# The sample tokens' state updates moved from the GDN and retention mixers into the feed-forward layers behind them

## The chip, the cores and the metric

The kernel runs on one core of a Trainium2 chip. A time is the device time of one execution in microseconds (us). The five engines are TensorE (PE; its weight loads are PEld), VectorE (DVE), ScalarE (ACT), GpSimd (POOL) and SyncE (SP). Each takes its own list of instructions strictly in order, and a DMA is issued by one of these lists.

## The reference

One step of a four-layer decoder over 264 tokens: 256 of a prompt and 8 sample tokens, each of another sequence. The mixers of the layers are pooling, gated DeltaNet (GDN), retention, pooling; behind each stands a SwiGLU feed-forward layer, and each sublayer ends in a layer norm. What the change touches are the new states of the 8 sample tokens, which are outputs:

```python
# GDN, per head (dk = dv = 128) and sample token
S = S * gl_n[..., None, None] + einsum('bhcd,bhce->bhde', kg_n, v_new)
# retention, per head (dk = 128, dv = 256)
S = gC[:, None, None] * S + einsum('bhcd,bhce->bhde', kz_n, v_n)
# feed-forward
a, b = split(x @ w13, 2); y = (silu(a) * b) @ w2
```

For a sample token a chunk is one token, so the new state is the old one times a decay plus an outer product of a key and a value. GDN has 8 heads of 8 states of 128x128 (0.52 MB a head, 4.2 MB in all), retention 8 heads of 8 states of 128x256 (1.05 MB a head, 8.4 MB in all). Nothing later in this step reads the new states; the mixers read the old ones, for the sample tokens' outputs.

## The kernel before

Activations lie with the 1024 features on partitions (8 blocks of 128) and the 264 tokens along the free axis. Each weight comes as float32 in chunks of 1 MB over SP's queue (`chunk`, three `raw` buffers); ACT casts it to a rounded high part (L198), DVE subtracts it from the raw chunk for the low part (L199), and each product is three matmuls (`mm3`, L123): high by high, high by low, low by high. The halves of a chunk have three buffers for each part, and the matmul results four PSUM buffers.

A feed-forward layer (`ffn`) runs over j = 0 to 21 blocks of w13 and then over 11 chunks of w2. The first eight j (`ND`) work on the activations before the layer norm, so that TensorE needn't wait for it. For them the norm is put in afterwards (`unfold`): DVE multiplies the product by 1/sigma (L396), ACT makes a correction u (L395), and POOL adds it (L397). Meanwhile `apply` makes the normed x of each block (L383, DVE L385, POOL L386, L387, L388). `evac` then gives silu(a)*b and its two parts (L413 to L416). The statistics of the norm come once, behind j = 0 (`stats`, L348 to L367): its vv is L355 on DVE. From j = 8 on only L198, L199 and `evac` are left. Here j = 0 to 7 are called the first phase, the rest the second.

In GDN (`sample`, `updates`), ACT's queue loads the states of two heads (`st`); TensorE multiplies each state with the key and the query of its token; `vn` and `vs` (8x128) follow on DVE, and `vs` goes to DRAM (`vd`, L930). `updates` brings `vd` back, one copy for each partition (`vbc`, one buffer, L938). POOL multiplies `st` by the decay (L940), DVE adds key by value with one instruction for each token (L948); for heads 4 to 7 POOL does half of the tokens (L943, L944). SP stores the result. `updates` runs for heads 0 to 3 behind the first half of the chain, woven into projections (`weave`), and for heads 4 to 7 in the output projection.

In retention the same stands in `chain`, per head: ACT multiplies by the decay (L1229), `vbc` comes in two halves (L1232), DVE adds (L1235), SP stores.

A scheduler of the framework places the instructions on each engine by its own timeline of estimated durations, so an instruction can stand far from where the code has it; `keep_in_program_order` fixes an instruction against its neighbours in the code on that engine. A buffer is reused once its last reader is done; for a stored tile that is the end of its store.

## Time and profile before

| | |
|---|---|
| three runs | 1429.88, 1430.71, 1433.75 us; median 1430.71 |
| the profiled execution | 1427.95 us, of it the span 1426.2 us |
| granted TensorE clock, mean | 0.973 |
| busy: PE, DVE, ACT, POOL | 1337.8 (94%), 1069.2 (75%), 821.6 (58%), 477.5 us (33%) |
| moved by DMA | 244.48 MB, of it 210.59 on SP's queue and 32.13 on ACT's; POOL issues none |

PE is busy in nearly the whole span, so a part of the kernel takes as long as its matmuls, plus the time in which they wait, plus what a clock below 1.00 adds. The stages that matter here are GDN with its updates (397 to 500 us), the feed-forward layer of layer 1 (first phase about 530 to 575, second to 700), retention (766 to 945) and the feed-forward layer of layer 2 (first phase about 1000 to 1043, second to 1175).

### The profile page before, as it was taken

The numbers are of one execution on the slowest core, as the hardware profiler recorded it, in microseconds if no ns is written. First come the engines' busy times: TensorE is split into PE (matmuls) and PEld (weight loads), VectorE is DVE, ScalarE is ACT, GpSimd is POOL, SyncE is SP. The second block draws the span as 40 slices with busy tenths as digits, with TensorE's granted clock in tenths as the row PEclk, the third lists the DMA queues.
The fourth block names the chain that finished last, engine by engine and source line by source line (L and its number), as shares of the span: only waits on it lengthen the run. The fifth ranks groups of instructions, "written<-read, shape, count | busy, mean of one in ns | idle before, by whom it ended". The sixth has DMA issues, their size and how long they took to land. (4 is left out here: it accounts for less than half of the span.)

```text
span 1426.2 us, 27556 instructions
## 1 busy us (share of the span) xinstructions
PE 1337.8 (94%) x10509; PEld 1281.1 (90%) x10509; DVE 1069.2 (75%) x2059; ACT 821.6 (58%) x1883; POOL 477.5 (33%) x517
## 2 busy tenths in 40 slices
...
GB/s 225 119 180 180 178 183 193 148 60 90 90 164 134 171 178 148 181 180 174 189 207 135 296 287 294 243 189 171 153 203 178 156 200 85 124 182 179 182 182 46
DMA packets 44341, 244.48 MB, mean 171 GB/s; under 512 B 5040, under 2 KB 9776, under 8 KB 18608
## 3 DMA queue, kind: packets, MB, share of 16 engines
q1 hardware_dynamic: 34784, 210.59, 42.2%
q10 hardware_dynamic: 9424, 32.13, 6.2%
...
q14 instruction: 51, 0.42, 0.1%
HBM read 225.86 MB, written 16.84 MB: 170 GB/s over the span
## 5 line engine op out<-in xcount | busy, mean ns | idle before, releaser
L199 DVE TENSOR_TENSOR l<-raw,h 128x512 fp32r<-128x512 f32 x658 | 470.7, 749 | 152.2 <-ACT h L198 147.1
L198 ACT CAST h<-raw 128x512 fp32r<-128x512 f32 x680 | 387.7, 617 | 237.8 <-PE mm L123 190.7
L123 PE MATMUL mm<-xh,h 128*128 128x264 f32 x1216 | 349.1, 289 | 11.0 <-DVE qk L1137 4.3
L123 PE MATMUL mm<-xl,h 128*128 128x264 f32 x1216 | 349.4, 288 | 2.7 <-DVE xl L388 2.7
L123 PE MATMUL mm<-xh,l 128*128 128x264 f32 x1216 | 347.1, 287 | 0.0
L123 PEld LDWEIGHTS mm<-xh,h 128*128 128x128 f32 x1216 | 230.9, 191 | 13.9 <-ACT xh L387 4.8
L123 PEld LDWEIGHTS mm<-xl,h 128*128 128x128 f32 x1216 | 230.9, 190 | 3.6 <-DVE xl L388 2.9
L123 PEld LDWEIGHTS mm<-xh,l 128*128 128x128 f32 x1216 | 230.3, 190 | 0.4
L123 PE MATMUL mm<-gh,l 128*128 128x264 f32 x704 | 200.7, 285 | 0.0
L123 PE MATMUL mm<-gh,h 128*128 128x264 f32 x704 | 200.3, 285 | 0.0
L123 PE MATMUL mm<-gl,h 128*128 128x264 f32 x704 | 198.7, 282 | 0.0
L123 PE MATMUL mm<-zh,l 128*128 128x266 f32 x496 | 141.9, 290 | 3.2 <-DVE l L199 3.1
L123 PE MATMUL mm<-zh,h 128*128 128x266 f32 x496 | 142.6, 292 | 1.8 <-DVE ab L396 1.6
L306 POOL TENSOR_TENSOR s<-d 128x264 f32<-128x264 f32 x6 | 5.7, 945 | 412.7 <-DVE d L290 412.7
L123 PE MATMUL mm<-zl,h 128*128 128x266 f32 x496 | 143.5, 290 | 0.2 <-DVE zl L293 0.2
L123 PEld LDWEIGHTS mm<-gh,h 128*128 128x128 f32 x704 | 132.5, 188 | 0.1
L123 PEld LDWEIGHTS mm<-gh,l 128*128 128x128 f32 x704 | 132.5, 188 | 0.1
L123 PEld LDWEIGHTS mm<-gl,h 128*128 128x128 f32 x704 | 132.5, 188 | 0.0
L123 PE MATMUL mm<-xh,w 128*128 128x264 f32 x416 | 111.1, 320 | 4.6 <-DVE ab L396 2.1
L397 POOL TENSOR_TENSOR ab<-ab,u 128x264 f32<-128x264 f32 x68 | 67.8, 1007 | 136.2 <-DVE ab L396 46.1
L123 PEld LDWEIGHTS mm<-zh,l 128*128 128x128 f32 x496 | 93.7, 190 | 4.3 <-DVE l L199 3.8
L123 PEld LDWEIGHTS mm<-zh,h 128*128 128x128 f32 x496 | 93.4, 190 | 3.6 <-DVE ab L396 2.7
...
## 6 DMA issues: line engine op xcount, KB each, us to landing
raw<-in_w_dram SPq DMA_DIRECT2D x132, 1024.0 KB, 4.9
raw<-in_rwi_dram SPq DMA_DIRECT2D x24, 1024.0 KB, 6.8
raw<-in_gwi_dram SPq DMA_DIRECT2D x16, 1024.0 KB, 4.8
vbc<-vd ACTq DMA_DIRECT2D x24, 512.0 KB, 4.4
st<-in_rst_dram ACTq DMA_DIRECT2D x8, 1024.0 KB, 12.2
out_ret_s_dram<-st SPq DMA_DIRECT2D x8, 1024.0 KB
raw<-in_rwo_dram SPq DMA_DIRECT2D x8, 1024.0 KB, 4.8
...
```

The costliest lines, as they stand in the source:

```text
L123: i = nc.tensor.matmul(*a, **k)
L198: S.copy(hi[:, w], src_ap[:, w])
L199: (E or V).tensor_tensor(lo[:, w], src_ap[:, w], hi[:, w].bitcast(F32), SUB)
L306: G.tensor_tensor(self.s1, d[:, self.seen[0]], d[:, m], ADD)
L397: (E or G).tensor_tensor(out, out, u[:n], ADD)
```

## The change

`updates` and its like in `chain` are gone. The mixers keep the keys and decays (`ksg`, `egs`, `ksr`) and write the values to DRAM (`vdg`, `vdr`). Two generators, `gdn_states` and `ret_states`, are made in the feed-forward layers of layers 1 and 2, and take a step at each j from 8 on and at each chunk of w2. A head loads its old states anew (`st`, L418 or L433), loads the broadcast values (`vbc`, L419 or L434), multiplies by the decay on ACT (64 instructions of 128x128 for GDN, L421; 32 of 128x512 for retention, L437), adds on DVE (64 of 128x128, L422; 64 of 128x256, L438), and stores (L425, L441). All its DMAs stand on POOL's queue; `st` and `vbc` have two buffers each, so head h+2 loads `st` when the store of head h is done. The loads of the old states in the mixers stay. Lines from L158 on move: L199 is L206 after, L355 L362, L396 L403, L397 L404, L385 L392, L416 L456, L433 (the load of ACT's table for the logarithm) L474.

```diff
--- before.py
+++ after.py
@@ -157,6 +157,13 @@
     gbh = pers.tile([P, 8, KB, 2], F32R, name="gbh")
     gbl = pers.tile([P, 8, KB, 2], F32R, name="gbl")
 
+
+    ksg = pers.tile([P, H, NB], F32, name="ksg")
+    egs = pers.tile([P, NB, H], F32, name="egs")
+    ksr = pers.tile([P, H, NB], F32, name="ksr")
+    vdg = drp.tile([H, NB, P], F32, tag="vdg", name="vdg", bufs=1)
+    vdr = drp.tile([H, NB, 256], F32, tag="vdr", name="vdr", bufs=1)
+
     wba = [pers.tile([P, 128], F32R, name="wba" + n) for n in "hl"]
 
     def small_loads():
@@ -403,10 +410,43 @@
             V.tensor_tensor(ln.d[:, m], ps, ln.d[:, m], ADD)
         ln.block(m)
 
+    def gdn_states(fp):
+
+        for h in range(H):
+            st = fp.tile([P, NB, P], F32, tag="st", name=nm("st"), bufs=2)
+            vbc = fp.tile([P, NB, P], F32, tag="vbc", name=nm("vbc"), bufs=2)
+            nc.gpsimd.dma_start(st, ap["gst"][h])
+            nc.gpsimd.dma_start(vbc, vdg[h].rearrange("b e -> (b e)").partition_broadcast(P).rearrange("p (b e) -> p b e", b=NB))
+            for b in range(NB):
+                S.mul(st[:, b], st[:, b], egs[:, b, h:h + 1])
+                V.scalar_tensor_tensor(st[:, b], vbc[:, b], ksg[:, h, b:b + 1], st[:, b], MUL, ADD)
+                if b % 4 == 3:
+                    if b > 4:
+                        nc.gpsimd.dma_start(ap["gdn_s"][h], st)
+                    yield
+
+    def ret_states(fp):
+
+        for h in range(H):
+            st = fp.tile([P, NB, 256], F32, tag="st", name=nm("st"), bufs=2)
+            vbc = fp.tile([P, NB, 256], F32, tag="vbc", name=nm("vbc"), bufs=2)
+            nc.gpsimd.dma_start(st, ap["rst"][h])
+            nc.gpsimd.dma_start(vbc, vdr[h].rearrange("b e -> (b e)").partition_broadcast(P).rearrange("p (b e) -> p b e", b=NB))
+            for b in range(NB):
+                if b % 2 == 0:
+                    S.mul(st[:, b:b + 2], st[:, b:b + 2], 1.0 - 2.0 ** (-5.0 - h))
+                V.scalar_tensor_tensor(st[:, b], vbc[:, b], ksr[:, h, b:b + 1], st[:, b], MUL, ADD)
+                if b % 4 == 3:
+                    if b > 4:
+                        nc.gpsimd.dma_start(ap["ret_s"][h], st)
+                    yield
+
     def ffn(l, pln):
         with tc.tile_pool(name=f"ffn{l}", bufs=1) as fp:
             gh = fp.tile([P, FB, T], F32R, name=nm("gh"))
             gl = fp.tile([P, FB, T], F32R, name=nm("gl"))
+
+            more = (gdn_states if l == 1 else ret_states)(fp) if l in (1, 2) else iter(())
 
             def evac(j, pa, pb):
                 s = fp.tile([P, T], F32, tag="s", name=nm("s"), bufs=2)
@@ -429,6 +469,7 @@
                 else:
                     pa, pb = proj2(ap["w13"][l, j], xh, xl)
                     evac(j, pa[:, 0:T], pb[:, 0:T])
+                    next(more, None)
             ln = LN(l * 2 + 1, l in (0, 1))
             tc.keep_in_program_order(S.preload_act_table_set("natural_log_exp_and_others"))
             hl = None
@@ -442,6 +483,9 @@
                 mm3(ps[:, 0:T], hl[(t % 16) // 8], (t % 8) * 128, 128, gh[:, k], gl[:, k], k == 0, k == FB - 1)
                 if k == FB - 1:
                     resid(ln, m, ps[:, 0:T])
+                if t % 16 == 8:
+                    next(more, None)
+            assert next(more, None) is None
             if not ln.defer:
                 ln.stats()
                 for m in range(KB):
@@ -714,14 +758,12 @@
                         ident[:NB, :NB].unsqueeze(2).to_broadcast([NB, NB, 8]), MUL)
         pse = sm_ps([P, NB, 8])
         PE.matmul(pse.rearrange("p b h -> p (b h)"), ones[:NB], gdg.rearrange("p b h -> p (b h)"), start=True, stop=True)
-        egs = gp.tile([P, NB, 8], F32, name="egs")
         V.tensor_copy(egs, pse)
 
         oht, ohs = [], {}
         hc = [(h, c) for h in range(2) for c in range(2)]
         idb = ident.unsqueeze(1).unsqueeze(1).to_broadcast([P, 2, 2, P])
         rks, rqs, brs, kgs, kbs, vbs, ats, tts, oss, oos = ({} for _ in range(10))
-        later = []
 
         def tile4(tag, bufs=1, dt=F32):
             return gp.tile([P, 2, 2, P], dt, tag=tag, name=nm(tag), bufs=bufs)
@@ -912,7 +954,6 @@
             V.scalar_tensor_tensor(sc[:, :, 0], egc[:NB, 2, h0:h0 + 2], -1.0, rk[:NB, :, 2], MUL, MUL)
             V.tensor_tensor(sc[:, :, 1], pqd[:NB], rk[:NB, :, 2], MUL)
             vn = gp.tile([NB, 2, P], F32, tag="vn", name=nm("vn"), bufs=2)
-            vd = drp.tile([2, NB, P], F32, tag="vd", name=nm("vd"))
             for h in range(2):
                 yield
                 hd = h0 + h
@@ -927,27 +968,7 @@
                 V.tensor_scalar(os_[:, h], pss[32:32 + NB], egc[:NB, 2, hd:hd + 1], None, MUL)
                 V.scalar_tensor_tensor(os_[:, h], vn[:, h], sc[:, h, 1:2], os_[:, h], MUL, ADD)
                 V.tensor_scalar(vs[:, h], vn[:, h], rk[:NB, h, 2:3], None, MUL)
-                nc.scalar.dma_start(vd[h], vs[:, h])
-                later.append((hd, st[2 * h:2 * h + 2], vd[h]))
-
-        def updates(n):
-
-            for _ in range(n):
-                hd, st, vd = later.pop(0)
-                vbc = gp.tile([P, NB, P], F32, tag="vbc", name=nm("vbc"), bufs=1)
-                nc.scalar.dma_start(vbc, vd.rearrange("b e -> (b e)").partition_broadcast(P).rearrange("p (b e) -> p b e", b=NB))
-                for i, s in enumerate(st):
-                    G.tensor_tensor(s, s, egs[:, 4 * i:4 * i + 4, hd:hd + 1].to_broadcast([P, 4, P]), MUL)
-                    if hd > 3 and i:
-                        vb, kc = vbc[:, 4 * i:4 * i + 4], kt[:, hd, TP + 4 * i:TP + 4 * i + 4]
-                        G.tensor_tensor(vb, vb, kc.unsqueeze(2).to_broadcast([P, 4, P]), MUL)
-                        G.tensor_tensor(s, s, vb, ADD)
-                    else:
-                        for b in range(4):
-                            bb = 4 * i + b
-                            V.scalar_tensor_tensor(s[:, b], vbc[:, bb], kt[:, hd, TP + bb:TP + bb + 1], s[:, b], MUL, ADD)
-                    nc.sync.dma_start(ap["gdn_s"][hd, :, 4 * i:4 * i + 4], s)
-                yield
+                nc.scalar.dma_start(vdg[hd], vs[:, h])
 
         def outputs(p):
 
@@ -1064,13 +1085,14 @@
             if p < 2:
                 for m in range(4 * p, 4 * p + 4):
                     pln.apply(m)
+        G.tensor_copy(ksg, kt[:, :, TP:T])
         for p in range(4):
             if p == 3:
                 drain(run(JOBS[0]))
             rks[p] = lengths([kt[:, 2 * p + h] for h in range(2)], "rk", ON_V[p])
         PE.pinned = True
         weave(turns(*(inverse(p) for p in range(4))), run(JOBS[1]), RATIO[0])
-        weave(seq(turns(operands(0), operands(1)), turns(sample(0), sample(1), outputs(0), outputs(1)), updates(4)), run(JOBS[2]), RATIO[1])
+        weave(seq(turns(operands(0), operands(1)), turns(sample(0), sample(1), outputs(0), outputs(1))), run(JOBS[2]), RATIO[1])
         weave(seq(turns(operands(2), operands(3), finish(0), finish(1)), turns(sample(2), sample(3), outputs(2), outputs(3))), run(len(jobs)), RATIO[2])
         PE.pinned = False
         pss, raws = {}, {}
@@ -1098,8 +1120,6 @@
             if c > 1:
                 half(c, 0)
             half(c, 1)
-            if c == 1:
-                drain(updates(4))
             for e, ps in enumerate(pss[c]):
                 resid(ln, 2 * c + e, ps[:, 0:T])
         return ln
@@ -1109,7 +1129,7 @@
         rope = rp.tile([P, 4, T], F32, name="rope")
         nc.scalar.dma_start(rope, ap["rope"])
         qd = [rp.tile([P, NB * 40], F32R, name=f"qd{i}") for i in range(2)]
-        zr = rp.tile([P, 4, 256], F32, tag="vbc", name="zr")[:, 0:2].rearrange("p a b -> p (a b)")[:, 0:NB * 40]
+        zr = rp.tile([P, NB * 40], F32, name="zr")
         G.memset(zr, 0.0)
         for t in qd:
             G.tensor_copy(t, zr)
@@ -1224,16 +1244,8 @@
             os_ = rp.tile([NB, 256], F32, tag="os", name=nm("os"), bufs=5)
             V.scalar_tensor_tensor(os_, vs, qs, pos[:NB], MUL, ADD)
             V.tensor_tensor(os_, os_, pos[32:32 + NB], ADD)
-            vd = drp.tile([NB, 256], F32, tag="vd", name=nm("vd"))
-            nc.scalar.dma_start(vd, vs)
-            S.mul(st, st, gam)
-            for half in range(2):
-                vbc = rp.tile([P, 4, 256], F32, tag="vbc", name=nm("vbc"), bufs=1)
-                nc.scalar.dma_start(vbc, vd[4 * half:4 * half + 4].rearrange("b e -> (b e)").partition_broadcast(P).rearrange("p (b e) -> p b e", b=4))
-                for b in range(4):
-                    bb = 4 * half + b
-                    V.scalar_tensor_tensor(st[:, bb], vbc[:, b], qk[:, 1, TP + bb:TP + bb + 1], st[:, bb], MUL, ADD)
-            nc.sync.dma_start(ap["ret_s"][h], st)
+            nc.scalar.dma_start(vdr[h], vs)
+            G.tensor_copy(ksr[:, h], qk[:, 1, TP:T])
 
 
             mv = rp.tile([P, 3, 2], F32, tag="mv", name=nm("mv"), bufs=2)
```

The scheduler does not leave these steps at j = 8 and later. On POOL, ahead of the feed-forward layer of layer 1, where L310 and L311 (after: L317 and L318) form the sums of the norm, stands before:

```order
236 L311 TENSOR_TENSOR s_966_6121<-s_966_6121,sq_6339 128x264
237 L311 TENSOR_TENSOR s_966_6121<-s_966_6121,sq_6347 128x264
238 L310 TENSOR_TENSOR s_965_6120<-s_965_6120,d_6119 128x264
239 L311 TENSOR_TENSOR s_966_6121<-s_966_6121,sq_6419 128x264
240 L397 TENSOR_TENSOR ab_6520<-ab_6520,u_6524 128x264
241 L397 TENSOR_TENSOR ab_6521<-ab_6521,u_6530 128x264
242 L386 TENSOR_TENSOR x<-y_6541,u_6539 128x264
```

and after the change:

```order
217 L419 DMA vbc_7302<-vdg 128x1024
218 L318 TENSOR_TENSOR s_958_6066<-s_958_6066,sq_6236 128x264
219 L317 TENSOR_TENSOR s_957_6065<-s_957_6065,d_6064 128x264
220 L318 TENSOR_TENSOR s_958_6066<-s_958_6066,sq_6244 128x264
221 L318 TENSOR_TENSOR s_958_6066<-s_958_6066,sq_6316 128x264
222 L425 DMA out_gdn_s_dram<-st_7142 128x1024
223 L419 DMA vbc_7461<-vdg 128x1024
224 L418 DMA st_7460<-in_gst_dram 128x1024
225 L425 DMA out_gdn_s_dram<-st_7301 128x1024
226 L419 DMA vbc_7620<-vdg 128x1024
227 L404 TENSOR_TENSOR ab_6417<-ab_6417,u_6421 128x264
228 L404 TENSOR_TENSOR ab_6418<-ab_6418,u_6427 128x264
```

The loads of heads 0 and 1 (L418, L419; `st_7142` and `st_7301` are their states) have moved in among the sums, and two stores (L425) and three more loads stand ahead of the first addition of `unfold` (L404). All 24 DMAs of the eight heads stand in front of POOL's last addition of the first phase. On DVE's list the last of the 64 L422 stands behind the fifth `gl` (L456) and ahead of the sixth.

On DVE at the start of the feed-forward layer of layer 2, where vv (L355) and the first products of `unfold` (L396) are made, stands before:

```order
1234 L355 SCALAR_TENSOR_TENSOR vv_12585<-sm_12578,t_12583 128x264
1235 L199 TENSOR_TENSOR l_12715<-raw_12712,h_12714 128x512 x2
1236 L199 TENSOR_TENSOR l_12721<-raw_12712,h_12720 128x512 x2
1237 L359 TENSOR_TENSOR t_12583<-r_12587 128x264
1238 L360 SCALAR_TENSOR_TENSOR t_12583<-t_12583,vv_12585 128x264
1239 L361 SCALAR_TENSOR_TENSOR r_12587<-t_12583,r_12587 128x264
1240 L199 TENSOR_TENSOR l_12805<-raw_12802,h_12804 128x512
1241 L365 TENSOR_TENSOR mr_12581<-mr_12581,r_12587 128x264
1242 L396 TENSOR_TENSOR ab_12596<-mm_12527,r_12587 128x264
1243 L396 TENSOR_TENSOR ab_12597<-mm_12528,r_12587 128x264
```

and after the change, with `st_13274` and `st_13429` as the states of heads 0 and 1:

```order
1216 L318 TENSOR_TENSOR s_1899_11882<-s_1899_11882,sq_12456 128x264
1217 L206 TENSOR_TENSOR l_12584<-raw_12575,h_12583 128x512 x2
1218 L438 SCALAR_TENSOR_TENSOR st_13274<-vbc_13275,ksr,st_13274 128x256 x6
1219 L362 SCALAR_TENSOR_TENSOR vv_12538<-sm_12531,t_12536 128x264
1220 L206 TENSOR_TENSOR l_12668<-raw_12665,h_12667 128x512
1221 L438 SCALAR_TENSOR_TENSOR st_13274<-vbc_13275,ksr,st_13274 128x256 x2
1222 L206 TENSOR_TENSOR l_12668<-raw_12665,h_12667 128x512
...
1234 L438 SCALAR_TENSOR_TENSOR st_13429<-vbc_13430,ksr,st_13429 128x256 x3
1235 L206 TENSOR_TENSOR l_12764<-raw_12755,h_12763 128x512
1236 L438 SCALAR_TENSOR_TENSOR st_13429<-vbc_13430,ksr,st_13429 128x256 x5
1237 L403 TENSOR_TENSOR ab_12639<-mm_12589,r_12540 128x264
```

Six of head 0's eight additions (L438) have moved ahead of vv (L362), and head 1's stand ahead of the products of j = 1 (L403, `ab_12639`). The last of the 64 L438 stands behind the 17th `gl`. POOL has the loads of these two heads right behind its two copies `zh` and `zl` (L281, L282 before), as its first DMAs.

On ACT the load of the logarithm's table (L433, after: L474) stands before behind the last silu of layer 1 (L413), and only casts of weights follow:

```order
738 L413 ACTIVATE s_8137<-mm_8087 128x264
739 L198 CAST h_8215<-raw_8213 128x512 x2
740 L415 CAST gh_6435<-s_8137 128x264
741 L433 ACT_TABLE_LOAD
742 L198 CAST h_8221<-raw_8213 128x512 x2
743 L198 CAST h_8279<-raw_8277 128x512 x2
```

After the change it stands in the first phase, ahead of a silu (L453) that loads its own table again, and the norm of the retention layer loads tables at L364 and L365:

```order
658 L421 ACTIVATE st_8096<-st_8096,egs 128x128 x8
659 L474 ACT_TABLE_LOAD
660 L402 ACTIVATE u_6871<-mr_6402,wc_6869 128x264
...
668 L453 ACT_TABLE_LOAD
669 L453 ACTIVATE s_6881<-ab_6867 128x264
...
796 L364 ACT_TABLE_LOAD
797 L364 ACTIVATE r_9059<-vv_9057 128x264
798 L365 ACT_TABLE_LOAD
799 L365 ACTIVATE r_9059<-r_9059 128x264
```

The preload was moved with head 6's multiplications (L421, `st_8096`), which stand ahead of it in the code; ACT has 18 table loads after the change and 14 before.

## Rows read from the trace of the kernel before

**Rows 1.** Windows by stage; columns in its first row, busy us and count per engine.

```profile
core 0: us, PE busy (x) PEld busy (x) DVE busy (x) ACT busy (x) POOL busy (x), PEclk, DMA share, GB/s
397.00:500.00 103.00, 85.37 (x624) 78.97 (x623) 82.10 (x195) 45.78 (x153) 56.79 (x67) 0.92 0.47 162
...
530.00:575.00 45.00, 42.74 (x335) 41.48 (x335) 42.21 (x73) 36.63 (x91) 23.84 (x27) 1.00 0.46 155
575.00:700.00 125.00, 125.00 (x1026) 124.94 (x1025) 76.43 (x132) 62.48 (x128) 9.46 (x10) 1.00 0.53 182
766.00:800.00 34.00, 26.61 (x196) 25.09 (x194) 27.61 (x56) 20.80 (x40) 18.17 (x17) 0.90 0.57 211
800.00:945.00 145.00, 141.96 (x1136) 136.31 (x1135) 131.33 (x276) 94.87 (x192) 69.46 (x56) 1.00 0.73 266
...
1000.00:1043.00 43.00, 41.62 (x327) 40.49 (x327) 40.98 (x72) 34.05 (x85) 20.64 (x23) 1.00 0.48 168
1043.00:1175.00 132.00, 132.00 (x1084) 131.94 (x1083) 75.25 (x129) 62.94 (x125) 13.97 (x15) 1.00 0.53 184
```

**Rows 2.** Chain that ended last, from the page, by engine.

```profile
PE 10%; ACT 0%; DVE 0%; issue 0%; ACTq 0%; DVEq 0%
```

**Rows 3.** VectorE groups in 397 to 500; columns as in section 5 of the page.

```profile
L948 DVE SCALAR_TENSOR_TENSOR st<-vbc,kt,st 128x128 f32<-128x128 f32 x48 | 27.9, 638 | 8.8 <-DMA vbc<-vd 8.8
```

**Rows 4.** GpSimd groups in the same stretch.

```profile
L940 POOL TENSOR_TENSOR st<-st,egs 128x512 f32<-128x512 f32 x12 | 13.2, 1109 | 2.4 <-PE sm L123 2.3
L944 POOL TENSOR_TENSOR st<-st,vbc 128x512 f32<-128x512 f32 x4 | 5.7, 1418 | 0.2
...
L943 POOL TENSOR_TENSOR vbc<-vbc,kt 128x512 f32<-128x512 f32 x4 | 4.4, 1089 | 8.3 <-DMA vbc<-vd 8.3
```

**Rows 5.** TensorE's waits in 397 to 500: us in all, times, longest.

```profile
PE sm L123 <- DVE os L927: 4.0, 2, 2.8
PE mm L123 <- ACT sz L1047: 3.1, 1, 3.1
```

**Rows 6.** TensorE's waits in 766 to 945.

```profile
PE mm L123 <- DVE qk L1137: 4.3, 1, 4.3
...
PE sm L123 <- POOL s L1219: 1.2, 1, 1.2
```

**Rows 7.** VectorE's updates of retention in 766 to 945.

```profile
L1235 DVE SCALAR_TENSOR_TENSOR st<-vbc,qk,st 128x256 f32<-128x256 f32 x64 | 36.9, 634 | 3.3 <-DMA vbc<-vd 2.6 <-ACT st L1229 0.7
```

**Rows 8.** Timeline of VectorE, 425 to 435: start, us, engine, line, operation.

```profile
429.78 1.65 DVE L948 SCALAR_TENSOR_TENSOR st<-vbc,kt,st 128x128 f32<-128x128 f32 x6
```

**Rows 9.** GpSimd's timeline ahead of layer 1's feed-forward.

```profile
519.39 0.76 POOL L311 TENSOR_TENSOR s<-s,sq 128x264 f32<-128x264 f32 x1
529.52 1.41 POOL L397 TENSOR_TENSOR ab<-ab,u 128x264 f32<-128x264 f32 x1 [9.38 <-ACT u L395]
```

**Rows 10.** VectorE's timeline in that feed-forward: fifth and sixth block.

```profile
556.65 0.42 DVE L416 TENSOR_TENSOR gl<-s,gh 128x264 fp32r<-128x264 f32 x1
...
562.81 0.42 DVE L416 TENSOR_TENSOR gl<-s,gh 128x264 fp32r<-128x264 f32 x1
```

**Rows 11.** Windows in retention, three slices of 20 us; columns as in rows 1.

```profile
820.00:840.00 20.00, 18.66 (x151) 17.78 (x151) 19.16 (x39) 13.15 (x28) 12.68 (x11) 1.00 0.71 272
840.00:860.00 20.00, 19.38 (x156) 18.46 (x155) 18.44 (x42) 13.39 (x29) 10.83 (x9) 1.00 0.88 324
```

**Rows 12.** DMA issues, from the page: KB each, median us to landing.

```profile
vbc<-vd ACTq DMA_DIRECT2D x24, 512.0 KB, 4.4
st<-in_rst_dram ACTq DMA_DIRECT2D x8, 1024.0 KB, 12.2
```

**Rows 13.** GpSimd's timeline ahead of layer 2's feed-forward.

```profile
976.63 0.20 POOL L282 CAST zl<-gbl 128x16 fp32r<-128x16 f32 x1
```

**Rows 14.** VectorE's timeline there, LN's vv, first unfolds, 17th block's gl.

```profile
987.90 0.43 DVE L355 SCALAR_TENSOR_TENSOR vv<-sm,t 128x264 f32<-128x264 f32 x1 [2.90 <-ACT h L198]
...
993.39 0.76 DVE L396 TENSOR_TENSOR ab<-mm,r 128x264 f32<-128x264 f32 x2
...
996.55 0.42 DVE L396 TENSOR_TENSOR ab<-mm,r 128x264 f32<-128x264 f32 x1
...
1085.53 0.43 DVE L416 TENSOR_TENSOR gl<-s,gh 128x264 fp32r<-128x264 f32 x1
```

**Rows 15.** Duration of a table load on ScalarE: min/median/max ns.

```profile
L433 ACT ACT_TABLE_LOAD  x4: 1283/1283/1283, 172.9 to 1348.9; - x4
```

**Rows 16.** A 128x128 operation of ScalarE, 397 to 500.

```profile
L1006 ACT ACTIVATE junk<-t 128x128 f32<-128x128 f32 x16 | 5.0, 311 | 4.7 <-DVE t L994 4.2
```

**Rows 17.** DMA issues of `vbc` on ScalarE's queue in retention: ns min/median/max.

```profile
L1232 ACTq DMA_DIRECT2D vbc<-vd x16: 326/330/353, 760.1 to 925.0; - x16
```

## The prediction, made before the changed kernel was run

> **What bounds the kernel now.** I read the chain that ended last first. TensorE is the only engine with a share worth naming in it [rows 2], so a part of the kernel takes its matmuls, plus the time in which they wait, plus what a lowered clock adds. The busy times by stage came next [rows 1]. In GDN's stage, 397 to 500 us, TensorE is busy 85.4 of 103 us, at a mean clock of 0.92, beside VectorE at 82.1 and GpSimd at 56.8. In retention it is idle 7.4 us of 766 to 800, at a clock of 0.90, and 3.0 us of 800 to 945. In the feed-forward layers the second phase has no idle time at all (125.0 of 125, 132.0 of 132) with VectorE under 62%, but in the first phase VectorE has next to no room: 42.2 busy of 45 us in layer 1, 41.0 of 43 in layer 2. So there is some time to win in GDN, little in retention, and the first phase is where an addition costs most. The changed kernel's order puts the work just there: all of GDN's states in the first phase and its approach, retention's from the approach to the 17th block.
>
> **Term A, GDN.** What goes there: 48 L948 on VectorE, 27.9 us busy and 8.8 us of waiting for `vbc` [rows 3]; on GpSimd 13.2 + 5.7 + 4.4 = 23.3 us and 8.3 us of waiting [rows 4]. The other 4 L940 lie ahead of the stage. TensorE loses 103 - 85.4 = 17.6 us by idling, and 85.4 x 0.08 = 6.8 us by clock, so 24.4 us is the most that can come back. No wait of TensorE names the updates; the largest name `os` of VectorE (4.0 us) and `sz` of ScalarE (3.1) [rows 5], both engines of a chain that the updates delay. Ends: 4 us, what `os` alone is worth, and 24.4 us. GDN's serial chain stays and weights must still be cast, so I take half: -12 us.
>
> **Term B, retention.** VectorE loses 64 L1235, 36.9 us busy and 3.3 idle [rows 7], ScalarE eight L1229. But TensorE's waits there name the start of the stage (`qk`, 4.3 us), with GpSimd's `s` at 1.2 [rows 6]. All its idle time is 10.4 us, and a full clock in 766 to 800 would return 26.6 x 0.10 = 2.7 more. Ends: 0 and 13; I take -4, since most of the idle time lies ahead of the work that goes. The store of each head leaves SP's queue, and a retention state buffer is free sooner; with 3 us of idle time from 800 on, that can bring no more than those.
>
> **Term C, feed-forward layer of layer 1.** Two things run beside each other here, and the larger one counts.
> VectorE: heads 2 to 7, 48 additions, stand within the first phase. Six beside a quiet GpSimd took 1.65 us, 0.275 each [rows 8]; within GDN's stage one was 27.9/48 = 0.58 us of busy time. So 13.2 to 27.9 us are added to an engine with 45 - 42.2 = 2.8 us of room: +10.4 to +25.1 us. ScalarE gains 64 multiplications of 0.31 us [rows 16], about 16 of the 64 for heads 0 and 1 ahead of the phase, so 48 x 0.31 + 1.3 for a table = 16.2 us, on 36.6 of 45: 52.8, which by itself would be +7.8.
> DMA: the first loads come behind L311 at 519.4, and the last additions follow the fifth `gl`, 556.7 to 562.8 [rows 9, 10]; say 40 us. By then eight `st` and eight `vbc` of 0.524 MB must be in, and six stores of 0.524 out (head 7 waits for head 5's), 11.5 MB, and weights at 155 GB/s, 6.2 MB [rows 1]. The best slice of the trace moves 324 GB/s at a DMA share of 0.88 [rows 11]: 17.7 MB take 54.6 us, +15. At 324/0.88 = 368 they take 48, +8; at the 272 GB/s of the slice before it, 65, +25. `vbc` takes 4.4 us to land and a 1.05 MB `st`, at these rates, 12.2 [rows 12]. Each head from the third on waits in series for a store, a load, eight multiplications (2.5 us) and eight additions (2.2 to 4.6), while the engine that waits holds casts and subtractions behind it, which TensorE needs: GpSimd's stores hold its unfold additions, ScalarE's multiplications the casts of weights.
> I take +14 us, range +8 to +27.
>
> The Trainium skill, page "DMA: Bandwidth & Descriptors", section "Issuing engines are not separate DMA queues", says that transfers started by any engine run on the same 16 DMA engines and interleave. By it GpSimd's queue brings no bandwidth of its own. That the trace agrees can be seen in retention: loads on ScalarE's queue land in 12.2 us while SP's weights run [rows 12]. If the rule did not hold, term C's DMA sum would fall away and VectorE's +10.4 would stand.
>
> **Term D, feed-forward layer of layer 2.** The first loads stand behind `zl` at 976.6 [rows 13]. Heads 0 and 1 need 2.1 MB each. With 324 - 168 = 156 GB/s left beside the weights [rows 1, 11] they land at about 990 and 1004. Then head 0 needs four multiplications and six additions ahead of vv, which was due at 987.9: about 996, 8 us late. Head 1 stands ahead of the products of j = 1, due at 996.6 behind those of j = 0 at 993.4 [rows 14]: about 1007, 10 us late, not on top of the 8. Four PSUM buffers hold two j, so TensorE stops soon after, and most of the 10 is lost.
> Then the whole: to the 17th `gl` at 1085.5 [rows 14], 109 us from the first load, 16 transfers in and 6 out of 1.05 MB are needed, 23.1 MB, and weights at about 174 GB/s, 19.0 MB. 42.1 MB take 130 us at 324 GB/s, +21; 114 at 368, +5; 155 at 272, +46. The first wait is part of that. VectorE's first phase gains heads 1 to 3, 24 additions of about 0.5, 12 us over 2 us of room, of which much falls into the same waits. From j = 8 on VectorE has 43% of room, so the additions themselves (32, 16 us) hide there; if a load is late they don't.
> I take +15, range +5 to +40.
>
> **Term E, tables.** Each table load is 1.28 us [rows 15]. Two of the four new ones stand in the serial chain of the retention layer's norm: +2.6 if TensorE then waits, 0 if its four PSUM buffers cover it. The other two are in C and D. I take +2.5.
>
> **The rest.** The copies of keys on GpSimd (one of 128x64, eight of 128x8) are small; GpSimd is 33% busy; 0, at most 3 us if they hold `s` in retention. GpSimd's issue of 24 DMAs in each feed-forward layer is not in the trace; an issue of `vbc` on ScalarE's queue is 0.33 us [rows 17]. In layer 1 24 x 0.33 = 8 us go into 21 us of room: nothing. The same bytes are stored as before; the old states are loaded a second time, 12.6 MB.
>
> Sum: -12 - 4 + 14 + 15 + 2.5 = +15.5 us on the profiled execution's 1427.95, that is 1443.5. The median of the runs shown is 2.8 us above that execution, so the forecast is 1446 us.
>
> **Rivals.**
> *The work hides, and the mixers' gain stays (faster).* For it: the second phases have VectorE and ScalarE half idle, and 182 GB/s is only half the DMA rate. It holds if transfers run near 368 GB/s and the additions cost 0.275 us. Then C +8, D +5, E 0; with A at -24 and B at -6 the sum is -17: 1414 us. Against it: the scheduler's order puts GDN's states into the phase with 2.8 us of room. It decides from the point where A and B pass C, D and E.
> *Gain and loss cancel.* A -12, B -4, C +10, D +5, E +1: 0, 1431 us.
> *The queues block each other (much slower).* A store on GpSimd's list holds all its later loads and additions, a load that isn't in holds ScalarE's casts. If transfers take what they take in the 272 GB/s slice, C is +25 and D +40; with A -8, B -2 and E +2.6 that is +58: 1488 us. For it: `st` at 12.2 us to landing where weights run at this rate. Against it: in the feed-forward layers the weights ask for 170 GB/s only, and when TensorE stops they ask for less. The same page of the Trainium skill (section "Anatomy of one DMA") gives 2.0 us plus the bytes at 436 GB/s for a transfer from this queue. By that a `st` of 1.05 MB would be an estimated 4.4 us alone, and D would lie at its low end.
> *The change doesn't move the work into the second phase.* That is so by the order, and counted in C and D. If the scheduler had left it at j = 8 and later, C would fall to the DMA's wait alone.
>
> **Chances.** My forecast's case 0.48 (1436 to 1465), the faster one 0.24, the one that cancels 0.14, the blocked one 0.14. About 4.3 us (0.3%) can't be told from no change. So faster 0.24, same 0.14, slower 0.62. The range reaches into the faster case, to 1416, and into the blocked one, to 1478, with about a tenth left out on each side.
>
> **What would show it.** For A: in GDN's stage TensorE's idle time falls from 17.6 to some 8 us, and VectorE's busy time by 28. For C and D: in the first phases TensorE idles by ten us or more, with waits named after `ab`, `x` or `h`, and VectorE's and ScalarE's own waits named after DMA of `st` or `vbc`; the granted clock falls behind the longest of them. DMA's share in them rises from 0.47 to 0.8 or more. E: two table loads in the norm of the retention layer, each ahead of `r`. The prediction is wrong if the first phases grow by less than 10 us each with TensorE above 90% busy (then the work hides), or if GDN's stage keeps its idle time (then the chain, not the updates, made it).

## The result, and the profile after

The changed kernel took 1440.01 us, the median of 8 runs (1435.27 to 1440.96), against 1430.84 us of the kernel before in the same runs: a ratio of 1.0069, 95% interval 1.0048 to 1.0090. It is slower by 0.7%, 10 us by the ratio. All ratios here are taken over the fast runs, without one execution of the kernel before that took 6950.61 us, so they differ a little from the quotients of the medians. The profiled execution took 1440.96 us (span 1438.9), 13.0 us above that of before.

| | before | after |
|---|---|---|
| busy: PE, DVE, ACT, POOL, us | 1337.8, 1069.2, 821.6, 477.5 | 1341.5, 1047.4, 846.0, 475.3 |
| moved by DMA, MB | 244.48 | 257.06 |
| granted TensorE clock, mean | 0.973 | 0.970 |

The whole is a small difference of large ones. To see them, the span is cut at points that TensorE passes in both kernels: the first product of a layer on `zh` (for a feed-forward layer that is the start of its first phase), and the first and the last of a w2 (on `gh`). A view of one tile shows them; here are `zh` and `gh` of layer 1's feed-forward layer after the change, with duration and first and last start.

```profile
L123 PE MATMUL mm<-zh,h x112: 280/287/561, 488.1 to 557.3; 128*128 128x266 f32 x112
```

```profile
L123 PE MATMUL mm<-gh,h x176: 281/284/290, 645.4 to 709.5; 128*128 128x264 f32 x176
```

So this layer's w13 part begins at 488.1 and ends at 645.4 us, 157.3 us; before it was 509.4 to 646.5, 137.1 us. All stages, and the same cuts for the kernels of the experiments (us, from one profiled execution of each; time in us, the median):

| kernel | time, ratio to before | GDN's layer to its feed-forward | w13 of layer 1 | w2 of layer 1 | retention | w13 of layer 2 | w2 of layer 2 |
|---|---|---|---|---|---|---|---|
| before | 1430.8 | 274.1 | 137.1 | 64.1 | 267.9 | 133.8 | 64.0 |
| after | 1440.0, 1.0069 | 252.1 | 157.3 | 64.1 | 257.5 | 158.7 | 64.1 |
| e1, GDN's part only | 1430.4, 0.9998 | 250.5 | 165.8 | 64.1 | 270.4 | 133.7 | 64.1 |
| e2, retention's part only | 1434.3, 1.0011 | 273.8 | 137.2 | 64.0 | 255.3 | 151.3 | 64.1 |
| e3, no new states | 1389.4, 0.9701 | 250.5 | 136.5 | 64.1 | 254.9 | 133.8 | 64.0 |
| e4, loads held back | 1418.5, 0.9905 | 252.1 | 145.0 | 70.4 | 257.1 | 140.5 | 65.7 |
| e5, pinned and spread | 1391.4, 0.9735 | 251.9 | 137.9 | 64.1 | 253.5 | 134.6 | 64.6 |
| e6, no loads past head 1 | 1440.2, 1.0072 | 250.5 | 156.6 | 64.1 | 258.1 | 159.2 | 64.0 |
| e7, no arithmetic | 1406.8, 0.9837 | 250.4 | 139.2 | 64.1 | 254.9 | 148.8 | 64.0 |
| e8, stores on SP | 1435.1, 1.0037 | 249.9 | 157.0 | 64.1 | 257.1 | 153.8 | 64.1 |
| e9, pinned only | 1400.9, 0.9792 | 250.5 | 140.3 | 64.0 | 254.8 | 138.1 | 65.2 |
| e10, e5 on SP's queue | 1394.0, 0.9738 | 252.1 | 137.2 | 64.1 | 255.2 | 135.4 | 64.6 |
| e11, before without additions | 1393.3, 0.9735 | 252.7 | 136.6 | 64.1 | 254.8 | 133.7 | 64.1 |
| e12, before without multiplications | 1421.4, 0.9932 | 270.3 | 137.1 | 64.1 | 265.3 | 133.7 | 64.1 |

After against before: GDN -22.0, w13 of layer 1 +20.2, retention -10.4, w13 of layer 2 +24.9, the rest within 1 us. That is +12.7, the difference of the spans.

These are the changed kernel's windows, to be read against [rows 1] (busy us and instructions of each engine, clock, DMA share, GB/s):

```profile
core 0: us, PE busy (x) PEld busy (x) DVE busy (x) ACT busy (x) POOL busy (x), PEclk, DMA share, GB/s
397.00:488.00 91.00, 88.16 (x719) 83.50 (x718) 64.50 (x160) 53.04 (x170) 38.77 (x55) 1.00 0.34 115
488.00:533.00 45.00, 34.71 (x246) 32.59 (x245) 39.91 (x88) 33.12 (x88) 19.81 (x29) 0.93 0.76 269
533.00:580.00 47.00, 39.19 (x283) 37.79 (x284) 43.86 (x94) 39.15 (x102) 23.17 (x30) 0.93 0.72 252
...
766.00:800.00 34.00, 32.66 (x266) 31.41 (x265) 25.87 (x57) 22.99 (x53) 27.50 (x25) 1.00 0.59 216
800.00:935.00 135.00, 135.00 (x1086) 130.44 (x1086) 100.02 (x211) 78.75 (x175) 61.19 (x55) 1.00 0.49 171
967.00:1010.00 43.00, 37.80 (x275) 36.77 (x275) 37.26 (x72) 30.99 (x72) 14.67 (x20) 0.92 0.91 348
1010.00:1053.00 43.00, 36.71 (x269) 36.07 (x269) 39.58 (x77) 31.44 (x73) 18.81 (x24) 0.92 0.83 313
1053.00:1126.00 73.00, 67.69 (x524) 66.67 (x523) 47.58 (x94) 40.19 (x80) 4.28 (x8) 0.95 0.74 274
```

In GDN's stage TensorE is now idle for 2.8 of 91 us at a full clock, where it was idle 17.6 of 103 at 0.92. In 766 to 800 it is busy 32.7 us at a full clock, where it was 26.6 at 0.90; from 800 on it has no idle time. In w13 of the two feed-forward layers it is the other way round: idle 10.3 and 7.8 us in layer 1, 5.2, 6.3 and 5.3 in layer 2 (the last of these in its second phase), and at clocks of 0.92 to 0.95, which adds some 5 and 9 us of slow matmuls. DMA's share has gone from 0.46 to 0.72 and more.

In layer 1 TensorE waits for VectorE's first products of unfold (waits in 488 to 580: us in all, times, longest):

```profile
PE mm L123 <- DVE ab L403: 14.0, 4, 6.3
```

VectorE's timeline shows what stands ahead of them (start, us, line, operation, idle time before with its releaser):

```profile
504.51 1.12 DVE L422 SCALAR_TENSOR_TENSOR st<-vbc,ksg,st 128x128 f32<-128x128 f32 x4
505.56 0.42 DVE L362 SCALAR_TENSOR_TENSOR vv<-sm,t 128x264 f32<-128x264 f32 x1
505.90 1.12 DVE L422 SCALAR_TENSOR_TENSOR st<-vbc,ksg,st 128x128 f32<-128x128 f32 x4
...
512.17 0.77 DVE L403 TENSOR_TENSOR ab<-mm,r 128x264 f32<-128x264 f32 x2
...
517.47 1.23 DVE L422 SCALAR_TENSOR_TENSOR st<-vbc,ksg,st 128x128 f32<-128x128 f32 x4 [3.23 <-ACT st L421]
518.61 0.42 DVE L403 TENSOR_TENSOR ab<-mm,r 128x264 f32<-128x264 f32 x1
```

Before, 4.3 us lay between vv and the first `ab` (523.3 to 527.6), and the second block's followed within 3 us. Now the norm's chain is threaded through the states: vv at 505.6, behind the additions of head 0 and half of head 1, the first `ab` at 512.2, and the second block's at 518.6 and 520.0, behind additions that wait for ScalarE, and ScalarE for a load:

```profile
517.03 1.28 ACT L421 ACTIVATE st<-st,egs 128x128 f32<-128x128 f32 x4 [3.63 <-DMA st<-in_gst_dram]
```

TensorE, with four PSUM buffers, stops at once (the two longest waits of this phase):

```profile
512.75 0.56 PE L123 MATMUL mm<-zh,h 128*128 128x266 f32 x1 [3.51 <-DVE ab L403]
...
534.10 0.56 PE L123 MATMUL mm<-zh,h 128*128 128x266 f32 x1 [6.35 <-DVE ab L403]
```

The 64 additions took 20.8 us of VectorE here, 0.325 us each, and 3.2 us of waiting; in GDN's stage it had been 0.58 [rows 3].

```profile
L422 DVE SCALAR_TENSOR_TENSOR st<-vbc,ksg,st 128x128 f32<-128x128 f32 x64 | 20.8, 382 | 3.2 <-ACT st L421 3.2
```

In layer 2 the waits go by other names, those of the casts and subtractions of weights (waits of TensorE, 967 to 1126):

```profile
PE mm L123 <- DVE l L206: 5.7, 2, 3.2
PE mm L123 <- ACT h L205: 5.3, 3, 4.0
PE mm L123 <- ACT gh L455: 3.0, 1, 3.0
```

No cast and no subtraction of this layer waits for a weight's transfer in this profile. What they stand behind is the state work. VectorE waits for head 0's `vbc` ahead of vv, and later a subtraction comes behind six of head 2's additions, with TensorE's second longest wait behind it:

```profile
978.76 2.46 DVE L438 SCALAR_TENSOR_TENSOR st<-vbc,ksr,st 128x256 f32<-128x256 f32 x6 [5.36 <-DMA vbc<-vdr]
...
1014.22 2.94 DVE L438 SCALAR_TENSOR_TENSOR st<-vbc,ksr,st 128x256 f32<-128x256 f32 x6
1017.09 1.28 DVE L206 TENSOR_TENSOR l<-raw,h 128x512 fp32r<-128x512 f32 x2
```

```profile
1017.82 0.58 PE L123 MATMUL mm<-zh,l 128*128 128x266 f32 x1 [3.24 <-DVE l L206]
```

The longest (4.0 us, to 1094.0) ends with a cast behind three multiplications of head 6 and the table load, and that for `gh` (3.0, to 1037.1) behind the eight additions of head 3.

The transfers there, from GpSimd's queue (KB each, median us to landing); before, half a `vbc` took 4.4 and `st` 12.2 [rows 12]:

```profile
st<-in_rst_dram POOLq DMA_DIRECT2D x8, 1024.0 KB, 8.1
vbc<-vdr POOLq DMA_DIRECT2D x8, 1024.0 KB, 10.3
out_ret_s_dram<-st POOLq DMA_DIRECT2D x8, 1024.0 KB, 5.5
```

In the norm of the retention layer the two table loads stand where the order put them, one ahead of each `r`:

```profile
717.78 1.28 ACT L364 ACT_TABLE_LOAD   x1
...
719.52 1.28 ACT L365 ACT_TABLE_LOAD   x1
```

### The profile page after: what moved, and what is told of

Same layout as the page of the kernel before. It is cut to its first block, busy times and chain, and to the rows that moved or that the text cites. A ratio compares the mean times of both kernels' runs of the same rounds, so it can differ in the third digit from the quotient of the medians.

```text
span 1438.9 us, 27678 instructions
## 1 busy us (share of the span) xinstructions
PE 1341.5 (93%) x10506; PEld 1284.2 (89%) x10509; DVE 1047.4 (73%) x2075; ACT 846.0 (59%) x1975; POOL 475.3 (33%) x550
## 2 busy tenths in 40 slices
DMA packets 44340, 257.06 MB, mean 179 GB/s; under 512 B 5040, under 2 KB 9776, under 8 KB 16560
## 5 line engine op out<-in xcount | busy, mean ns | idle before, releaser
L206 DVE TENSOR_TENSOR l<-raw,h 128x512 fp32r<-128x512 f32 x658 | 467.8, 746 | 151.4 <-ACT h L205 146.2
L123 PE MATMUL mm<-zh,h 128*128 128x266 f32 x496 | 146.4, 299 | 14.2 <-DVE ab L403 13.8
L123 PEld LDWEIGHTS mm<-zh,h 128*128 128x128 f32 x496 | 96.9, 197 | 16.2 <-issue 13.5
L404 POOL TENSOR_TENSOR ab<-ab,u 128x264 f32<-128x264 f32 x68 | 67.4, 1000 | 103.6 <-PE mm L123 40.4
## 6 DMA issues: line engine op xcount, KB each, us to landing
vbc<-vdr POOLq DMA_DIRECT2D x8, 1024.0 KB, 10.3
```

Of the source, the lines that this page charges most:

```text
L123: i = nc.tensor.matmul(*a, **k)
L206: (E or V).tensor_tensor(lo[:, w], src_ap[:, w], hi[:, w].bitcast(F32), SUB)
L404: (E or G).tensor_tensor(out, out, u[:n], ADD)
```

## The experiments

The theory after the result: the mixers gain what the whole state work cost there, and the feed-forward layers lose in their first phase, because the scheduler places the work among the norm's chain. The rivals: the transfers cost wherever they stand (bandwidth, the second load of the states), or GpSimd's queue does.

**e1 and e2: one mixer's part alone.** In e1 retention's code is that of before, in e2 GDN's.

```diff
-            more = (gdn_states if l == 1 else ret_states)(fp) if l in (1, 2) else iter(())
+            more = gdn_states(fp) if l == 1 else iter(())   # e1; e2: ret_states(fp) if l == 2
```

> Only GDN's state work is in the feed-forward layer; retention's stays in its mixer as before. My theory is that the change is two moves, each with its own gain and its own larger or equal loss in the first phase: by the milestones of TensorE GDN's stage won 22 us and the layer behind it lost 20. Then this kernel stands 2 us below the kernel before, plus the 2 to 3 us of two table loads in the retention layer's norm: between -3 and +3 us (ratio 0.998 to 1.002). The rival, that the loss behind GDN is the price of one general thing (a slower DMA or a lower clock through the kernel), would leave a smaller loss here and so a gain of 5 us or more.

> Only retention's state work is in the feed-forward layer; GDN's stays as before. By the same milestones retention won 13 us (10 with the tables' loss), and the layer behind it lost 25. Without GDN's part the two table loads in retention's norm are gone. So +12 us on the kernel before (ratio 1.008; 1.005 to 1.011). Rival: if retention's gain came from GDN's earlier end, it is less here and the kernel is 20 us slower or more.

Measured: e1 1430.43 us, 0.9998 (0.9982 to 1.0014), as expected: GDN's gain and its loss cancel. Its retention stage grew by 2.5 us with the mixer's code as before: that is the price of the two table loads. The other profiles agree: with these loads in the norm (after, e4, e6, e8) retention takes 257.1 to 258.1 us, without them (e2, e3, e7, e9) 254.8 to 255.3. e2: 1434.25 us, 1.0011 (0.9999 to 1.0023), where 1.005 to 1.011 was expected. Retention's gain was as expected (-12.6); w13 of layer 2 lost 17.5 and not 25. On VectorE's list the later heads stand at other places than after the whole change (head 6 behind the 14th `gl` here, behind the 16th there). So the loss of one layer is not a constant of its work. In e1's profile w13 of layer 1 lost 28.7 us with VectorE's additions at the same places as after the change; that execution was 5 us above the median of its runs. So the same order can differ by several us in a stage between two executions.

**e3: no new states.** The mixers of the changed kernel, nothing in the feed-forward layers.

```diff
-            more = (gdn_states if l == 1 else ret_states)(fp) if l in (1, 2) else iter(())
+            more = iter(())
```

> The changed kernel without any of the new work in the feed-forward layers: the sample tokens' new states are neither computed nor stored. The mixers are those of the changed kernel. My theory: both mixers keep their gain, 22 and 13 us, and the feed-forward layers are as before, so 35 us faster than the kernel before, 1395 us (1390 to 1400). Rival: the mixers' gain belongs in part to the moved order alone and is smaller or larger without the work, then 1405 or more.

Measured: 1389.43 us, 0.9701 (0.9684 to 0.9718). The mixers keep their gain (-23.6 and -13.0), the feed-forward layers are as before. 1389 us is what the state work, placed at no cost, would leave; the changed kernel gives back 50 us of it.

**e4: loads held back to the second phase.** A column of a finished block is copied into each buffer first, so that the load waits.

```diff
+            G.tensor_copy(st[:, 0, 0:1], gl[:, (8, 9, 11, 13, 15, 17, 19, 21)[h], 0:1].bitcast(F32))
             nc.gpsimd.dma_start(st, ap["gst"][h])
```

> The changed kernel with one addition: ahead of each head's state load GpSimd copies one column of a finished block of the layer into the state's buffer, so that the load waits for it. Heads start behind blocks 8, 9, 11, 13, 15, 17, 19, 21 in layer 1 and 7, 8, 10, 12, 14, 16, 18, 20 in layer 2, that is from the second phase on. My theory, that the loss comes from the first phase, where VectorE and the queues have no room, gives the mixers' gain with little loss: 1400 us (1395 to 1412), faster than the kernel before by 2%. Rival one, that the second load of the old states and the transfers are what costs wherever they stand: 1425 to 1440. Rival two, that GpSimd's DMAs slow VectorE and the weights in any phase: above 1420 as well, with idle time of TensorE in the second phase.

Measured: 1418.5 us, 0.9905 (0.9886 to 0.9924): out of the first phase the loss is halved, but not gone, so it is neither the theory's 1400 nor as much as the first rival's 1425, and just under the second's 1420, whose sign, idle time in the second phase, is there. Its waits in layer 1 behind the first phase show why:

```profile
ACT st L422 <- DMA st<-in_gst_dram: 12.3, 4, 6.3
...
PE mm L123 <- ACT h L205: 8.4, 3, 4.0
```

ScalarE's multiplications stand where the scheduler expected the load to be in and wait for it, 12.3 us in all, and the casts of weights stand behind them. So the phase is not all that counts: a multiplication must not stand ahead of its load's landing either.

**e5: multiplications pinned, and spread.** Each multiplication is kept behind the instruction ahead of it in the code, and the half heads are spread over w13's second phase and w2.

```diff
-                S.mul(st[:, b], st[:, b], egs[:, b, h:h + 1])
+                i = S.mul(st[:, b], st[:, b], egs[:, b, h:h + 1])
+                tc.keep_in_program_order(i)
...
                     pa, pb = proj2(ap["w13"][l, j], xh, xl)
+                    if j in (8, 10, 12, 14, 16, 18, 20):
+                        next(more, None)
                     evac(j, pa[:, 0:T], pb[:, 0:T])
-                    next(more, None)
...
-                if t % 16 == 8:
+                if t % 16 == 8 and t // 16 in range(10):
```

> The changed kernel with ScalarE's multiplications of the states pinned to their place in the code, and that place spread: one half head ahead of the silu of every second block from j = 8 to 20, the rest behind the first ten chunks of w2. The loads are free, so heads 0 and 1 come early and each later load has some 20 us before it is used. From the runs so far: with no states at all 1389, with loads held back to the second phase 1418.5, where TensorE waited most for ScalarE's casts, which stood behind multiplications whose load wasn't in. If it is that lead time that costs, this is 1390 to 1402. Rival, bandwidth: 12.6 MB more and the broadcasts cost wherever they stand, then 1410 to 1420 again.

Measured: 1391.44 us, 0.9735 (0.9719 to 0.9751). All of the work is done, from the same loads on the same queue, at 5 us more by the ratios than in the kernel that does none of it (0.9735 against 0.9701). The lead is less even than expected: the states of heads 0 and 1 are asked for 51 to 74 us ahead of their first multiplication, those of heads 2 to 4 20 to 27, and those of heads 5 to 7 only 8 to 15. Windows of layer 1's feed-forward (487 to 689) and layer 2's:

```profile
487.00:532.00 45.00, 43.00 (x324) 40.82 (x324) 42.44 (x75) 32.56 (x78) 20.73 (x25) 1.00 0.57 189
532.00:625.00 93.00, 91.89 (x741) 90.90 (x740) 70.80 (x142) 60.60 (x146) 15.88 (x22) 1.00 0.66 233
...
943.00:992.00 49.00, 48.58 (x385) 47.88 (x384) 45.68 (x81) 37.81 (x91) 19.53 (x23) 1.00 0.64 239
992.00:1077.00 85.00, 83.17 (x676) 82.62 (x675) 63.89 (x125) 52.98 (x112) 12.74 (x18) 1.00 0.78 296
1077.00:1142.00 65.00, 65.00 (x535) 64.87 (x534) 50.58 (x93) 39.33 (x72) 23.54 (x27) 1.00 0.90 350
```

In w2 of layer 2 the transfers reach 350 GB/s at a share of 0.90, and TensorE is busy for all of its 65 us. ScalarE is back to 14 table loads, since the last thing ahead of the preload in the code is now the cast (`gh`) behind the last silu. This version beats both kernels.

**e6 and e7: most loads left out, and the arithmetic left out.** e6 loads heads 0 and 1 only and works on their buffers for all eight; e7 loads and stores, and computes nothing.

```diff
+            if h < 2:                                     # e6
+                ...
+                two.append((st, vbc))
+            st, vbc = two[h % 2]
...
-                S.mul(st[:, b], st[:, b], egs[:, b, h:h + 1])     # e7
-                V.scalar_tensor_tensor(st[:, b], vbc[:, b], ksg[:, h, b:b + 1], st[:, b], MUL, ADD)
```

> The changed kernel without the loads of states and values of heads 2 to 7: these heads work on the buffers of heads 0 and 1, so the new states are wrong; the multiplications, additions and stores stay, and the scheduler puts them where it will. If the loss in the first phases is the wait for transfers (loads behind stores, and the engines behind them), 1405 to 1418 is left. If it is the time of VectorE and ScalarE in a phase with no room, it stays at 1430 to 1440.

> The changed kernel without the multiplications and additions: the states are loaded and stored as they are, so the new states are the old ones. All transfers of GpSimd's queue stay. If the additions and multiplications cost by the engines' time and by standing in line behind a transfer, 1389 to 1400. If the transfers themselves cost, by bandwidth taken from the weights or by holding GpSimd's additions of unfold, 1410 or more.

Measured: e6 1440.22 us, 1.0072 (1.0053 to 1.0090); e7 1406.76 us, 0.9837 (0.9821 to 0.9854), between the two that were expected. In layer 1 e7, the transfers without the arithmetic, loses 2.1 us, e6 19.5 and the changed kernel 20.2: without the arithmetic nearly all of the loss is gone. But e6 isn't the changed kernel's arithmetic by itself. The loads of heads 0 and 1 and all stores stay, and the scheduler packs the rest closer: heads 0 to 5 stand ahead of the first `gl`, where it was heads 0 to 2. Its VectorE shows the mechanism with no load of a state to wait for: 20 additions between vv and the first `ab`, which are 11 us apart (4.3 before, 6.6 with four additions after the change).

```profile
502.85 0.43 DVE L362 SCALAR_TENSOR_TENSOR vv<-sm,t 128x264 f32<-128x264 f32 x1
...
506.65 2.19 DVE L426 SCALAR_TENSOR_TENSOR st<-vbc,ksg,st 128x128 f32<-128x128 f32 x8
...
511.38 1.66 DVE L426 SCALAR_TENSOR_TENSOR st<-vbc,ksg,st 128x128 f32<-128x128 f32 x6
...
513.90 0.77 DVE L403 TENSOR_TENSOR ab<-mm,r 128x264 f32<-128x264 f32 x2
```

The delay of vv itself is another matter: in e7, with no addition at all, it comes 16.3 us behind the layer's first product, against 13.9 before and 17.5 after the change.

In layer 2 e6 loses 25.4 us, e7 15.0 and the changed kernel 24.9, and these are not shares of one loss. e6 has all eight heads ahead of the seventh `gl` (after the change the last is behind the 17th), and it keeps the wait of 5.4 us for head 0's `vbc`. In e7 TensorE waits for the casts:

```profile
PE mm L123 <- ACT h L205: 11.3, 5, 5.4
```

```profile
970.00:1010.00 40.00, 31.57 (x219) 30.61 (x220) 30.93 (x54) 26.27 (x65) 19.91 (x28) 0.87 0.92 357
```

But no cast waits for a weight there. On ScalarE they stand behind `xh` (L394), which waits for GpSimd's `x` (L393), and `x` stands on GpSimd's list behind loads that wait for an earlier transfer. The cast behind this `xh` ends the longest wait, 5.4 us, at 974.5:

```profile
971.64 0.58 POOL L431 DMA_DIRECT2D st<-in_rst_dram  x1 [1.66 <-DMA out_ret_s_dram<-st]
972.24 0.75 POOL L393 TENSOR_TENSOR x<-y,u 128x264 f32<-128x264 f32 x1
```

```profile
973.02 0.41 ACT L394 CAST xh<-x 128x264 fp32r<-128x264 f32 x1 [2.10 <-POOL x L393]
```

So what e7 shows in layer 2 is GpSimd's list, and not bandwidth taken from the weights. A part of it is e7's own: loads of `vbc` wait 9.1 us for the one before them, since no addition stands between. How much of this is in the changed kernel's 24.9, no run shows.

**e8 and e10: another queue.** e8 is the changed kernel with the stores on SP's queue, e10 is e5 with all its DMAs of states on SP's queue.

```diff
-                        nc.gpsimd.dma_start(ap["gdn_s"][h], st)
+                        nc.sync.dma_start(ap["gdn_s"][h], st)
```

> The changed kernel with the stores of the new states on SP's queue instead of GpSimd's. A store waits for VectorE's additions; on GpSimd it holds unfold's additions, on SP it holds the loads of weights. If GpSimd's line is what costs, 1420 to 1432; if it is the waits on ScalarE and VectorE for the loads, no change beyond 6 us around 1440; a much slower run (1450 and more) would show the weights held.

> The pinned and spread kernel with all its DMAs of states on SP's queue instead of GpSimd's. A store that waits for VectorE, or a load that waits for a store, now holds the weights behind it. If GpSimd's queue is needed because its line has nothing behind that TensorE needs in the second phase, this is slower by 3 to 15 us than 1391. If the place of the work alone matters, it is within 3 us of 1391.

Measured: e8 1435.07 us, 1.0037 (1.0024 to 1.0049), the loss of layer 1 the same to 0.3 us, that of layer 2 smaller by 4.9. The stores on GpSimd's list are not what costs in layer 1; in layer 2 they, or the other order that the move gave, are a fifth. e10: 1394.04 us, 0.9738 (0.9710 to 0.9766), not to be told from e5's 0.9735. Where the place is right, the queue is free to choose.

**e9: pinned only.** The half heads stay at each block from j = 8 to 21, as in the changed kernel's code.

```diff
-                    if j in (8, 10, 12, 14, 16, 18, 20):     # against e5
+                    if j in range(8, 22):
```

> As the pinned and spread kernel, but with the half heads where the changed kernel's code has them: at each block from j = 8 to 21, the last two behind chunks of w2. So only the pin is new against the changed kernel. If standing in the first phase was all that cost, 1391 to 1396, as with the spread. If transfers bind too where they come dense, retention's 25 MB in some 90 us beside 184 GB/s of weights ask for more than the 410 GB/s that the changed kernel's best slice showed: then layer 2's feed-forward loses 10 us or more, and the whole is 1401 to 1412.

Measured: 1400.86 us, 0.9792 (0.9767 to 0.9817). The pin is worth 39 us of the 49 between the changed kernel and e5. The time is just at the edge of what the bandwidth theory gave, but w13 of layer 2 lost only 4.3 us of the 10 it asked for, and w13 of layer 1 lost 3.2. Against e5 these are 3.5 and 2.4 us, and the tail behind the last cut, whose code is the same in all kernels, gives another 2.7. Weights do come late here, if little: casts of layer 2 wait 3.0 us in all for them, where the changed kernel's wait for none. Between a load's issue and its head's first multiplication lie 6 to 9 us for heads 2 to 7 of layer 1, and ScalarE waits for none of them, so 20 us of lead are not needed there. In the dense stretch of layer 2 TensorE has no idle time even where DMA's share is full:

```profile
1030.00:1050.00 20.00, 20.00 (x165) 20.00 (x164) 15.84 (x33) 12.20 (x25) 2.67 (x5) 1.00 1.00 397
1050.00:1070.00 20.00, 20.00 (x166) 20.00 (x165) 15.17 (x30) 12.48 (x26) 1.60 (x3) 1.00 1.01 426
```

**e11 and e12: the kernel before without additions, without multiplications.** e11 leaves out the broadcasts and the additions (GpSimd's half of them too), e12 the multiplications by the decay.

```diff
-                            V.scalar_tensor_tensor(s[:, b], vbc[:, bb], kt[:, hd, TP + bb:TP + bb + 1], s[:, b], MUL, ADD)   # e11
...
-                    G.tensor_tensor(s, s, egs[:, 4 * i:4 * i + 4, hd:hd + 1].to_broadcast([P, 4, P]), MUL)   # e12
-            S.mul(st, st, gam)
```

> The kernel before, without the broadcasts of the values and the additions in both mixers (VectorE's, and GpSimd's half of them for GDN's heads 4 to 7): the states are only multiplied by their decay and stored. My theory is that VectorE's 37 us of additions and waits are what made GDN's stage long: it gives 16 to 22 of GDN's 23 us, and 8 to 12 of retention's 13, so 1397 to 1407. Rival: GpSimd's and ScalarE's multiplications, which stand in front of casts, are the larger part; then 1412 or more.

> The kernel before without the multiplications by the decay in both mixers (GpSimd's 16 in GDN, ScalarE's 8 in retention); broadcasts, additions and stores stay, on the old states. By my theory this gives little: 1422 to 1430. By the rival, 1412 or less, with retention's stage shorter by 6 us or more.

Measured: e11 1393.27 us, 0.9735 (0.9712 to 0.9758), somewhat more than was expected; e12 1421.35 us, 0.9932 (0.9909 to 0.9954). Without broadcasts and additions GDN loses 21.4 and retention 13.1 us, all but 2 of what the whole removal gives in these stages (e3); the multiplications are worth 3.8 and 2.6. In e11's GDN stage TensorE is idle for 3.5 of 91 us, though GpSimd still has 51.5 us of work:

```profile
397.00:488.00 91.00, 87.51 (x700) 82.55 (x699) 70.29 (x162) 52.75 (x170) 51.48 (x66) 0.98 0.44 152
```

## Why the prediction was right, point by point

The direction, the time (1446 forecast, 1440 measured) and the mechanism held: the mixers gain, the first phases lose more, and the order showed it ahead of the run. But four of the five terms were larger than I took them: the gains together by 19 us, the losses by 16. That the sum came out at +12.7 us, by the spans, where I had +15.5, is luck in the sizes.

- **Term A, GDN: -12 taken, -22.0 measured.** The step "GDN's serial chain stays and weights must still be cast, so I take half" failed. Nearly all of the 24.4 us of lost time came back. TensorE's waits for `os` (L927), `sz` and `cs` name a chain, but they were the updates' doing: in e11, with broadcasts and additions gone, they are gone too. VectorE's list held the chain's next step behind additions, the first of which waited for `vbc`; TensorE's wait then names the chain's tile, never the update:

```profile
401.97 4.66 DVE L948 SCALAR_TENSOR_TENSOR st<-vbc,kt,st 128x128 f32<-128x128 f32 x8 [1.73 <-DMA vbc<-vd]
...
406.92 0.34 DVE L927 TENSOR_SCALAR os<-sm,egc 8x128 f32<-8x128 f32 x1
```

```profile
407.41 0.68 PE L123 MATMUL sm<-s,t 128*128 128x128 f32 x4 [2.79 <-DVE os L927]
```

How much of the 22 us is the additions' own time and how much their wait for the broadcast, no run separates.

- **Term B, retention: -4 taken, -12.9 measured** (-10.4 with the tables' +2.5). The step "most of the idle time lies ahead of the work that goes" failed: by e11 broadcasts and additions make all 13. The first updates stand at 769 to 781 us, and the `qk` that TensorE waits for [rows 6] comes behind them on VectorE's list:

```profile
777.47 3.69 DVE L1235 SCALAR_TENSOR_TENSOR st<-vbc,qk,st 128x256 f32<-128x256 f32 x4 [2.58 <-DMA vbc<-vd]
...
783.59 0.75 DVE L1137 TENSOR_TENSOR qk<-mm,rope 128x264 f32<-128x264 f32 x2
```

My upper end, 13, was right.

- **Term C, layer 1: +14 taken, +20.2 measured, range +8 to +27.** VectorE's sum (+10.4 to +25.1) held what was measured, and the DMA's (+15) was the wrong one: e7's transfers cost +2.1. What I had not priced is that the additions stand inside the norm's chain, which all first products wait for.
- **Term D, layer 2: +15 taken, +24.9 measured, range +5 to +40.** The first wait came as worked out, but shorter: VectorE idles 5.4 us for head 0's `vbc`, and vv comes 4.8 us late and not 8 (at 981.1, 13.8 us behind the first product; before it was 9.0). The second step, that the bytes of the whole stretch make up the rest, isn't in the trace: no cast waits for a weight, and the three longest waits of TensorE stand behind a head's additions or multiplications. I had counted the engines' own part into the first waits.
- **The ceiling of DMA was wrong.** I took 324 GB/s, and 368 at a full share, from one slice [rows 11]. e9 moved 426 GB/s over 20 us at a share of 1.01. A slice in which nothing asks for more says nothing of a ceiling.
- **Term E, tables: +2.5 taken, +2.5 measured** (e1).
- **GpSimd's queue.** An issue holds GpSimd for 0.57 us in the median, not the 0.33 of ScalarE's queue [rows 17]:

```profile
L418 POOL DMA_DIRECT2D st<-in_gst_dram x8: 527/567/797, 489.8 to 552.6; - x8
```

In layer 1 it was as harmless as said (e8); in layer 2 e8 took 4.9 us off. What the Trainium skill's page "DMA: Bandwidth & Descriptors" has in "Issuing engines are not separate DMA queues" agrees with e5 and e10: 0.9735 and 0.9738 with GpSimd's queue and with SP's. Its formula in "Anatomy of one DMA", an estimated 4.4 us for 1.05 MB, lies under what `st` took beside the weights, 8.1.
- **The rivals.** "The work hides" is what e5 does, at 1391 us and not 1414; the changed kernel doesn't, because its order doesn't leave the work in the second phase. "The queues block each other" is what e7 shows in layer 2, with +15 and nothing to compute. After the change the loss there is +25 and not +40, and e8 speaks against GpSimd's stores as its main cause.

What stays open: why layer 2 loses 7 us more after the whole change (24.9) than with retention's part alone (17.5). The two differ in the order from head 4 on; no run separates that from the timing of the transfers, or from the several us by which e1's stage differed with the same order. How the 24.9 divide between the engines' time and GpSimd's list stays open as well.
